# Weight pieces of a hybrid diffusion step: eight 128-row chunks in two buffers instead of four chunks in four

## The chip, the cores and the metric

The kernel runs on one core of a Trainium2 chip. The metric is the device time of one execution in microseconds (us); three runs of the kernel before were timed, and the profile is of a further execution of the same program. About 0.2% of the time is what a measurement of this kernel can tell from no change.

## The reference, cut to what matters

One inference step over two layers. 128 context tokens and 512 latent tokens (640 columns in all) go through the same weights. Each layer multiplies the normalised input by one wide matrix, sends the slices of the result through three kinds of mixer, and multiplies the concatenated results by an output matrix.

```python
mod = jnp.matmul(jax.nn.silu(cond), w_ada) + b_ada
shift, scale, gate = jnp.split(mod[:, None, :], 3, axis=-1)
h = rmsnorm(x, norm_g) * (1 + scale) + shift
proj = jnp.matmul(h, w_in)                       # 2048 -> 7168
q, k, v, ag, lx, lg, hv, hx1, hx0, hg = jnp.split(proj, SPLITS, axis=-1)
...
xc = dwconv(lx, lru_conv_w, lru_conv_b, 2, 1)
h_f = rglru_dir(xc, lru_wa[0], ..., False)       # 64x64 block gates, then a scan
h_b = rglru_dir(xc, lru_wa[1], ..., True)
...
out = jnp.matmul(jnp.concatenate([att, lru, hy], axis=-1), w_out)   # 2048 -> 2048
return x + gate * out, k_store, v_store, h_last
```

## The kernel before, in words

All activations lie transposed: 128 features on the partitions, 640 tokens in the free dimension, sixteen such tiles for 2048 features, each kept as a high and a low part (`A`, type fp32r) so that three matmuls give nearly fp32 precision. TensorE multiplies in fp32r; the weights come from memory as fp32 and are split the same way.

**A weight piece.** `load_w` (L369) fetches four chunks of 128 rows by 128 columns with one DMA of 256 KB into a tile `wr`, ScalarE casts it to fp32r (`wh`, L178), and VectorE subtracts to get the rest (`wl`, L179). `wr`, `wh` and `wl` have four buffers each, in the pool `W` (L145) and by `WR = 4` (L37).

**A projection.** `gemm` (L401) makes one block of 128 output features: over sixteen chunks, that is four pieces, each chunk with three weight/input pairs (`wh` with the high part, `wh` with the low part, `wl` with the high part) in two halves of 320 tokens. So a piece is 24 matmuls and a projection is 96, all at L420. Two PSUM accumulators alternate. Between the pieces the loop may call `hook`, which spreads the next adaLN product over VectorE (L335), and `filt`, which spreads the filter and convolution steps.

**Order.** A scheduler places the instructions of each engine at build time by priority and by its own estimate of when they are ready; every engine then works through its own list in order, and so do the DMA queues (nearly all transfers are issued by SP). The calls of `load_w` in `gemm` and `gemm_parts` stand under `high_priority(offset=600)`, so that a piece is fetched and split ahead of the matmuls that use it. A buffer is given again when its last reader is done: for `wr` that is the subtraction, for `wh` and `wl` the last matmul of the piece.

**Stages**, once per layer: adaLN and normalisation (layer 0: forty smaller pieces of two or four chunks, `gemm_part`, L513, called from L1265); the hyena gates; the RG-LRU (`lru`, L926, four blocks j); attention (`attention`, L1037, eight heads); three attention gates; hyena's inputs, filters and convolutions with the other gates; the output projection (`out_proj`, L1365). Its last two feature blocks, and the first two of the next layer, go through `gemm_parts` (L379), which runs over the tokens in two parts and keeps the pieces of a pool `wz` for both.

**The RG-LRU block** matters below. `lru` makes two projections, LX and LG, then builds the block-diagonal gate weights in a tile of the same tags: GpSimd clears `wr` (L950), four small DMAs fill it (L954), and it is split like a piece (L957). Four sets of six matmuls (L713, through `mm3`) read its `wh` and `wl`: two gates for the forward scan, two for the backward one. They stand between the matmuls of the next projection, since each set waits for ScalarE to empty the one PSUM tile `pS` of the set before (L968).

Of the kernel before, what the change touches and what calls it, by code (L numbers as in the profile page):

```python
# [11 lines left out]
F32 = mybir.dt.float32  # L12
F32R = mybir.dt.float32r
# [20 lines left out]
EPS = 1e-6  # L34
TCE_W = 258
PI = math.pi
WR = 4  # L37
CVB = 3
LEAD = 4
NAT = 4  # L40
# [97 lines left out]
class K:  # L138
    def __init__(self, ctx, tc, i, o, taps=None):
        self.ctx, self.tc, self.nc, self.i, self.o = ctx, tc, tc.nc, i, o  # L140
        self.taps = taps or {}
        nc = tc.nc
        P = lambda name, bufs, **kw: ctx.enter_context(tc.tile_pool(name=name, bufs=bufs, **kw))
        self.cst = P("cst", 1)
        self.W = P("W", 4)  # L145
        self.sm = P("sm", 2)
        self.pm = P("pm", 2, space=PSUM)
        self.hook = self.filt = None
        self.hn = 0
        self.n = 0  # L150
# [215 lines left out]
                nc.vector.scalar_tensor_tensor(mod[:, sl, s], mod[:, sl, s], 1.0, g, op0=ALU.add, op1=ALU.mult)  # L366


    def load_w(self, wd, k, m0, n=4, keep=None):  # L369

        nc = self.nc
        wr = self.tl(self.W, [128, 4, 128], F32, "wr", bufs=WR)[:, :n, :]
        nc.sync.dma_start(wr, wd[k * 128:(k + n) * 128, m0:m0 + 128].rearrange("(c p) m -> p c m", p=128))
        wh = self.tl(keep or self.W, [128, 4, 128], F32R, "wh")[:, :n, :]
        wl = self.tl(keep or self.W, [128, 4, 128], F32R, "wl")[:, :n, :]
        self.split(wh, wl, wr)
        return wh, wl

    def gemm_parts(self, wd, ms, rhs, order, parts, keeps):  # L379

        nc = self.nc
        ps = [self.pm.tile([128, 2, 512], F32, name=self.nm("g_%d" % m), tag="m") for m in ms]
        ws = {}
        yield ps
        for n0, (c0, c1, j, o) in enumerate(parts):
            for a in range(4):
                ks = order[4 * a:4 * a + 4]
                for m, p in zip(ms, ps):
                    if n0 == 0:
                        with self.tc.high_priority(offset=600):  # L390
                            ws[a, m] = self.load_w(wd, ks[0], m, keep=keeps[a])
                        if self.hook is not None:
                            next(self.hook, None)
                    wh, wl = ws[a, m]
                    for c, k in enumerate(ks):
                        for n, (w, x) in enumerate(((wh, 0), (wh, 1), (wl, 0))):
                            nc.tensor.matmul(p[:, j, o:o + c1 - c0], lhsT=w[:, c, :], rhs=rhs[k][x][:, c0:c1],  # L397
                                             start=(a == 0 and c == 0 and n == 0), stop=(a == 3 and c == 3 and n == 2))
                yield

    def gemm(self, wd, ms, rhs, order=range(KC)):  # L401

        nc = self.nc
        ps = [self.pm.tile([128, 2, 512], F32, name=self.nm("g_%d" % m), tag="m") for m in ms]
        for a in range(4):
            ks = order[4 * a:4 * a + 4]
            for m, p in zip(ms, ps):
                with self.tc.high_priority(offset=600):
                    wh, wl = self.load_w(wd, ks[0], m)
                if self.hook is not None:  # L410
                    self.hn += self.hr
                    while self.hn >= 1:
                        self.hn -= 1
                        next(self.hook, None)
                if self.filt is not None and (a + 1) * self.fs // 4 > a * self.fs // 4:
                    next(self.filt, None)
                for c, k in enumerate(ks):
                    for n, (w, x) in enumerate(((wh, 0), (wh, 1), (wl, 0))):
                        for j in range(2):
                            nc.tensor.matmul(p[:, j, :HT], lhsT=w[:, c, :], rhs=rhs[k][x][:, j * HT:(j + 1) * HT],  # L420
                                             start=(a == 0 and c == 0 and n == 0), stop=(a == 3 and c == 3 and n == 2))
        return [p[:, :, :HT] for p in ps]
# [503 lines left out]
    def lru(self, l, hs, j, pool, hl_tile):  # L926
# [19 lines left out]
        xl = self.tl(pool, [128, 644], F32R, tag="lxl")  # L946
        self.split(xh, xl, xc)
        sg = self.silu2(self.proj(l, COL_LG + j * 128, hs), pool, "lsg", 1)
        wr = self.tl(self.W, [128, 4, 128], F32, "wr", bufs=WR)
        nc.gpsimd.memset(wr, 0.0)  # L950
        for gi, nmw in ((0, "lru_wa"), (1, "lru_wi")):
            for bl in range(2):
                s = slice(bl * 64, bl * 64 + 64)
                nc.sync.dma_start(wr[s, 2 * gi:2 * gi + 2, s], i[nmw][l, :, 2 * j + bl].rearrange("d c e -> c d e"))  # L954
        wh = self.tl(self.W, [128, 4, 128], F32R, "wh")
        wl = self.tl(self.W, [128, 4, 128], F32R, "wl")
        self.split(wh, wl, wr)  # L957
        hh = []
        for d in range(2):
# [240 lines left out]
    def run(self):  # L1200
# [12 lines left out]
        with ExitStack() as st, self.tc.tile_pool(name="ps0", bufs=1, space=PSUM) as self.pst:  # L1213
# [12 lines left out]
            hs = []  # L1226
# [34 lines left out]
            for gi, (k0, kn) in enumerate(groups):  # L1261
                more = gi + 1 < len(groups)
                nxt = iter(())
                for n, m0 in enumerate(first):
                    self.gemm_part(self.load_w(w, k0, m0, kn), m0, hs, k0, kn, self.early[0, m0])  # L1265
                    ada_to(done + (2 if kn == 4 or gi else 1))
                    next(nxt, None)
                    if more and n == NAT:
# [96 lines left out]
    def out_proj(self, l):  # L1365
# [3 lines left out]
        self.hr = RATE[l]["out"]  # L1369
        wd, mod, ms = self.i["w_out"][l], self.par[l]["mod"], self.mix  # L1370
        zs = ExitStack()
        zp = zs.enter_context(self.pool("wz", 8))
        st = ExitStack()
        pool = st.enter_context(self.pool("out"))
        acc = self.tl(pool, [128, T], tag="acc")
# [173 lines left out]
```

## Time and profile before

| | |
|---|---|
| median of three runs | 2725.28 us (2720.43 to 2726.11) |
| the profiled execution | 2730.49 us, of which 2728.5 us from first to last instruction |
| TensorE busy / its weight loads | 95% / 91% of the span |
| VectorE / ScalarE / GpSimd busy | 70% / 39% / 10% |
| granted TensorE clock, mean | 0.987 of full speed |
| DMA moved | 354.83 MB, 130 GB/s |

Matmuls are pipelined, so their recorded lengths overlap; the engine's rate is read from the distance between starts. "Idle before" an instruction is the time its engine did nothing ahead of it, and the releaser is whatever ended last of what it waited for. Idle time of an engine that is not the bound costs nothing.

### The profile page before, as it was taken

Reading aid. Unit: us, or ns where it says so; the run is one execution under the profiler, and the core shown is the slowest. Engines: PE = TensorE matmul, PEld = TensorE weight load, DVE = VectorE, ACT = ScalarE, POOL = GpSimd, SP = SyncE. Lnnn points to the kernel's source line nnn. Section 1 sums busy time; section 2 is a strip of 40 time slices with the busy share of each in tenths; the row PEclk is TensorE's granted clock in tenths of the full one; section 3 lists DMA queues with packets and bytes.
Section 4 is the critical chain, followed back from the end, with each engine's and each line's share of the span. In section 5 each row is a group of like instructions: output and inputs, shape, how many; then the busy total and the mean of one; then the engine's idle time right before and its main releaser. Section 6 shows DMA issues by size and latency. Waiting matters only on the chain. (4 is left out here: it accounts for less than half of the span.)

```text
span 2728.5 us, 45802 instructions
## 1 busy us (share of the span) xinstructions
PE 2599.8 (95%) x17503; PEld 2485.5 (91%) x17503; DVE 1920.0 (70%) x3499; ACT 1076.9 (39%) x1970; POOL 261.6 (10%) x352
## 2 busy tenths in 40 slices
PE   4999989999999999989998999999999999999998
PEld 2589989999999998889998999999999999989997
DVE  3568997787888787777679467877777756564333
ACT  4224545455554222132235256444455522223222
POOL 1000220000000221200001012000000021120000
PEclk9999999999999999999999999999999999999999
DMA  8773443332333545576664323422322252345333
GB/s 256 247 239 118 128 136 90 90 106 66 102 93 114 173 136 158 158 227 200 191 196 147 117 69 86 127 87 86 101 75 64 59 166 79 106 143 158 98 94 118
DMA packets 439911, 354.83 MB, mean 130 GB/s; under 512 B 26746, under 2 KB 367618, under 8 KB 439436
## 3 DMA queue, kind: packets, MB, share of 16 engines
q1 hardware_dynamic: 428618, 336.39, 41.1%
q10 hardware_dynamic: 9586, 9.42, 1.1%
q0 software_dynamic: 1488, 6.10, 0.6%
q8 instruction: 137, 2.24, 0.3%
q14 instruction: 82, 0.67, 0.1%
HBM read 316.51 MB, written 35.32 MB: 129 GB/s over the span
## 5 line engine op out<-in xcount | busy, mean ns | idle before, releaser
L420 PE MATMUL g<-A,wh 128*128 128x320 f32 x8320 | 1614.1, 311 | 5.6 <-ACT A L178 5.0
L420 PEld LDWEIGHTS g<-A,wh 128*128 128x128 f32 x8320 | 1321.3, 189 | 7.3 <-ACT A L178 5.3
L420 PE MATMUL g<-A,wl 128*128 128x320 f32 x4160 | 963.9, 310 | 0.0
L178 ACT CAST wh<-wr 128x512 fp32r<-128x512 f32 (+1 forms) x592 | 362.1, 613 | 966.3 <-PE g L420 696.2
L420 PEld LDWEIGHTS g<-A,wl 128*128 128x128 f32 x4160 | 702.6, 189 | 0.2
L179 DVE TENSOR_TENSOR wl<-wr,wh 128x512 fp32r<-128x512 f32 (+1 forms) x592 | 429.2, 728 | 339.0 <-ACT wh L178 323.9
L335 DVE SCALAR_TENSOR_TENSOR adas<-wa,cs,adas 128x512 f32<-128x512 f32 x480 | 363.9, 784 | 61.4 <-DMA wa<-in_w_ada 60.1
L1160 ACT ACTIVATE e<-e,mx 128x768 f32<-128x768 f32 (+1 forms) x160 | 133.7, 835 | 69.2 <-DVE e L1159 68.9
L1159 DVE TENSOR_SCALAR_CACHE_REDUCE e<-pS 128x768 f32<-128x768 f32 (+1 forms) x160 | 131.0, 819 | 9.1 <-PE pS L713 3.9
L1122 POOL TENSOR_TENSOR oq<-ot 128x640 f32<-128x640 f32 x16 | 20.9, 1309 | 912.5 <-ACT ot L1118 689.7
L713 PE MATMUL pS<-kk,qq 128*128 128x384 f32 (+1 forms) x288 | 100.3, 348 | 3.9 <-DVE e L1159 3.4
L521 PE MATMUL gp<-A,wh 128*128 128x320 f32 x512 | 101.9, 318 | 1.0 <-ACT wh L178 1.0
L397 PE MATMUL g<-A,wh 128*128 128x320 f32 (+2 forms) x384 | 92.9, 324 | 8.9 <-DVE A L492 5.9
L521 PEld LDWEIGHTS gp<-A,wh 128*128 128x128 f32 x512 | 79.7, 189 | 23.0 <-issue 11.2
L713 PE MATMUL pS<-kl,qq 128*128 128x384 f32 (+1 forms) x288 | 95.2, 331 | 0.0
L179 DVE TENSOR_TENSOR wtl<-pt,wth 128x512 fp32r<-128x512 f32 (+1 forms) x144 | 70.1, 522 | 29.6 <-ACT wth L178 29.3
L178 ACT CAST wth<-pt 128x512 fp32r<-128x512 f32 (+1 forms) x144 | 59.7, 459 | 61.6 <-PE pt L1103 60.0
L313 PE MATMUL pa<-wada,csw 128*32 128x512 f32 (+1 forms) x320 | 52.7, 565 | 28.9 <-DVE st L436 21.5
L397 PEld LDWEIGHTS g<-A,wh 128*128 128x128 f32 x384 | 67.0, 194 | 14.4 <-DVE A L492 8.3
L1396 DVE SCALAR_TENSOR_TENSOR xf<-g,mod,xo 128x128 f32<-128x128 f32 (+3 forms) x96 | 38.3, 432 | 55.8 <-PE g L420 23.2
L1166 DVE SCALAR_TENSOR_TENSOR e<-e,rz,e 128x768 f32<-128x768 f32 (+1 forms) x80 | 70.6, 882 | 1.7
L713 PEld LDWEIGHTS pS<-kk,qq 128*128 128x128 f32 x288 | 54.0, 187 | 14.7 <-DVE e L1159 8.8
(353 smaller groups left out, 3159.7 us busy)
## 6 DMA issues: line engine op xcount, KB each, us to landing
wr<-in_w_in SPq DMA_DIRECT2D x440, 256.0 KB
wa<-in_w_ada SPq DMA_DIRECT2D x256, 256.0 KB
wada<-in_w_ada SPq DMA_DIRECT2D x64, 512.0 KB
wr<-in_w_out SPq DMA_DIRECT2D x128, 256.0 KB
mx<-md SPq DMA_DIRECT2D x28, 320.0 KB
md<-ot SPq DMA_DIRECT2D x16, 320.0 KB
gm<-md SPq DMA_DIRECT2D x16, 320.0 KB
R<-rd SPq DMA_DIRECT2D x16, 320.0 KB
```

Of the source, the lines that this page charges most:

```text
L178: self.nc.scalar.copy(hi, src)
L179: self.nc.vector.tensor_tensor(lo, src, hi.bitcast(F32), op=ALU.subtract)
L313: nc.tensor.matmul(acc[32 * q:32 * q + 32, :], lhsT=self.csw[:, k, :], rhs=w[:, j, :], start=k < 4, stop=k >= 12, tile_position=(0, 32 * q))
L335: nc.vector.scalar_tensor_tensor(acc[:, s], w, c, acc[:, s], op0=ALU.mult, op1=ALU.add)
L397: nc.tensor.matmul(p[:, j, o:o + c1 - c0], lhsT=w[:, c, :], rhs=rhs[k][x][:, c0:c1], start=(a == 0 and c == 0 and n == 0), stop=(a == 3 an ...
L420: nc.tensor.matmul(p[:, j, :HT], lhsT=w[:, c, :], rhs=rhs[k][x][:, j * HT:(j + 1) * HT], start=(a == 0 and c == 0 and n == 0), stop=(a == ...
L521: nc.tensor.matmul(p[:, j, :HT], lhsT=w[:, c, :], rhs=rhs[k0 + c][x][:, j * HT:(j + 1) * HT], start=(c == 0 and t == 0), stop=(c == n - 1 ...
L713: self.nc.tensor.matmul(out, lhsT=a, rhs=b, start=(n == 0), stop=(n == len(pairs) - 1))
L1159: V.tensor_scalar(e[:, :nk].rearrange("p (a b) -> p a b", a=nhf), ps[:, :nhf, :hw], -1.0, None, op0=ALU.mult, op1=ALU.min, accum_out=mx)
L1160: nc.scalar.activation(e[:, :nk], e[:, :nk], AF.Exp, scale=-1.0, bias=mx, accum_out=Z[:, c:c + 1])
L1166: V.scalar_tensor_tensor(es[0][:, :nk], es[1][:, :nk], rz[:, 1:2], es[0][:, :nk], op0=ALU.mult, op1=ALU.add)
L1396: V.scalar_tensor_tensor(x[:, a:b], p, mod[:, 32 + m, s:s + 1], xo[:, a:b], op0=ALU.mult, op1=ALU.add)
```

## The change

`load_w` takes a list of piece starts and fetches each with a DMA of its own into one tile of eight chunks, then casts and subtracts the whole tile in one instruction each. `gemm` and `gemm_parts` call it at every second piece and hand out halves. The pool `W` has two buffers of eight chunks in place of four of four (the same bytes), and `wz` four in place of eight. The forty early pieces and the RG-LRU's gate weights, which have at most four chunks, now take a part of an eight-chunk buffer each. The calls of `hook` and `filt` stay at every piece of four chunks.

```diff
-WR = 4
-        self.W = P("W", 4)
+        self.W = P("W", 2)
...
-    def load_w(self, wd, k, m0, n=4, keep=None):
+    def load_w(self, wd, ks, m0, n=4, keep=None):
         nc = self.nc
-        wr = self.tl(self.W, [128, 4, 128], F32, "wr", bufs=WR)[:, :n, :]
-        nc.sync.dma_start(wr, wd[k * 128:(k + n) * 128, m0:m0 + 128].rearrange("(c p) m -> p c m", p=128))
-        wh = self.tl(keep or self.W, [128, 4, 128], F32R, "wh")[:, :n, :]
-        wl = self.tl(keep or self.W, [128, 4, 128], F32R, "wl")[:, :n, :]
+        N = n * len(ks)
+        wr = self.tl(self.W, [128, 8, 128], F32, "wr")[:, :N, :]
+        for j, k in enumerate(ks):
+            nc.sync.dma_start(wr[:, j * n:j * n + n, :], wd[k * 128:(k + n) * 128, m0:m0 + 128].rearrange("(c p) m -> p c m", p=128))
+        wh = self.tl(keep or self.W, [128, 8, 128], F32R, "wh")[:, :N, :]
+        wl = self.tl(keep or self.W, [128, 8, 128], F32R, "wl")[:, :N, :]
         self.split(wh, wl, wr)
         return wh, wl
...
     def gemm(self, wd, ms, rhs, order=range(KC)):
+        ws = {}
         for a in range(4):
             ks = order[4 * a:4 * a + 4]
             for m, p in zip(ms, ps):
-                with self.tc.high_priority(offset=600):
-                    wh, wl = self.load_w(wd, ks[0], m)
+                if a % 2 == 0:
+                    with self.tc.high_priority(offset=600):
+                        ws[m] = self.load_w(wd, (ks[0], order[4 * a + 4]), m)
+                wh, wl = (w[:, a % 2 * 4:a % 2 * 4 + 4, :] for w in ws[m])
...
     def lru(self, l, hs, j, pool, hl_tile):
-        wr = self.tl(self.W, [128, 4, 128], F32, "wr", bufs=WR)
+        wr = self.tl(self.W, [128, 8, 128], F32, "wr")[:, :4, :]
-        wh = self.tl(self.W, [128, 4, 128], F32R, "wh")
-        wl = self.tl(self.W, [128, 4, 128], F32R, "wl")
+        wh = self.tl(self.W, [128, 8, 128], F32R, "wh")[:, :4, :]
+        wl = self.tl(self.W, [128, 8, 128], F32R, "wl")[:, :4, :]
...
-                    self.gemm_part(self.load_w(w, k0, m0, kn), m0, hs, k0, kn, self.early[0, m0])
+                    self.gemm_part(self.load_w(w, (k0,), m0, kn), m0, hs, k0, kn, self.early[0, m0])
...
-        zp = zs.enter_context(self.pool("wz", 8))
+        zp = zs.enter_context(self.pool("wz", 4))
```

`gemm_parts` changes as `gemm` does: a load at every even a, halves handed to a and a + 1.

## Rows read from the trace of the kernel before

**Rows 1.** The page, busy time, share of the span and instructions of each engine.

```profile
PE 2599.8 (95%) x17503; PEld 2485.5 (91%) x17503; DVE 1920.0 (70%) x3499; ACT 1076.9 (39%) x1970; POOL 261.6 (10%) x352
```

**Rows 2.** Busy time by stage: RG-LRU 0, attention 0, hyena 0, RG-LRU 1, attention 1.

```profile
core 0: us, PE busy (x) PEld busy (x) DVE busy (x) ACT busy (x) POOL busy (x), PEclk, DMA share, GB/s
256.00:412.00 156.00, 140.58 (x911) 137.96 (x910) 142.12 (x207) 81.03 (x111) 36.02 (x30) 0.95 0.42 125
412.00:886.00 474.00, 467.02 (x3176) 452.67 (x3175) 384.81 (x752) 245.09 (x473) 25.64 (x16) 1.00 0.32 93
886.00:1228.00 342.00, 319.36 (x2164) 310.26 (x2163) 266.55 (x439) 84.99 (x157) 59.38 (x92) 0.98 0.56 171
1592.00:1730.00 138.00, 135.09 (x905) 133.53 (x904) 102.35 (x156) 81.25 (x112) 33.78 (x30) 0.99 0.30 89
1730.00:2190.00 460.00, 452.81 (x3064) 438.19 (x3063) 352.16 (x702) 236.65 (x462) 24.89 (x16) 0.99 0.28 82
```

**Rows 3.** Waits: who waited for whom, us in total, times, longest us.

```profile
ACT wh L178 <- PE g L420: 696.2, 308, 8.5
DVE wl L179 <- ACT wh L178: 323.9, 188, 5.1
...
PE pt L775 <- DVE uS L771: 11.8, 8, 2.3
...
PE g L420 <- ACT A L178: 5.0, 1, 5.0
```

**Rows 4.** Groups by line and form: xcount, busy us, mean ns of one, idle before.

```profile
L179 DVE TENSOR_TENSOR wl<-wr,wh 128x512 fp32r<-128x512 f32 x576 | 422.6, 736 | 332.0 <-ACT wh L178 317.1 <-PE pt L341 8.8 <-DMA wr<-in_w_in 2.5
L178 ACT CAST wh<-wr 128x512 fp32r<-128x512 f32 x576 | 355.6, 619 | 957.2 <-PE g L420 696.2 <-issue 94.5 <-PE gp L521 44.1
...
L179 DVE TENSOR_TENSOR kl<-ks,kk 64x896 fp32r<-64x896 f32 x32 | 34.7, 1085 | 11.8 <-ACT kk L178 11.5
...
L178 ACT CAST kk<-ks 64x896 fp32r<-64x896 f32 x32 | 30.1, 941 | 14.2 <-DVE ks L1035 13.8
```

**Rows 5.** Output projection of layer 1: chain (start, us), then timelines of ACT and DVE.

```profile
2507.02 3.52 PE g L420 x24
...
2532.84 0.62 ACT L178 CAST wh<-wr 128x512 fp32r<-128x512 f32 x1 [2.90 <-PE g L420]
2533.49 0.69 DVE L179 TENSOR_TENSOR wl<-wr,wh 128x512 fp32r<-128x512 f32 x1 [2.83 <-ACT wh L178]
```

**Rows 6.** Timelines of ACT, DVE and PE, one RG-LRU block of layer 1.

```profile
1608.40 0.62 ACT L178 CAST wh<-wr 128x512 fp32r<-128x512 f32 x1 [2.23 <-POOL lt L986]
1612.50 0.69 DVE L179 TENSOR_TENSOR wl<-wr,wh 128x512 fp32r<-128x512 f32 x1
1618.72 0.45 PE L420 MATMUL g<-A,wl 128*128 128x320 f32 x2
1624.86 0.61 ACT L178 CAST wh<-wr 128x512 fp32r<-128x512 f32 x1
1631.45 0.31 PE L713 MATMUL pS<-lxh,wl 128*128 128x322 f32 x1
```

**Rows 7.** The same timelines, last RG-LRU block of layer 0.

```profile
351.83 0.64 ACT L178 CAST wh<-wr 128x512 fp32r<-128x512 f32 x1
360.12 1.28 DVE L179 TENSOR_TENSOR wl<-wr,wh 128x512 fp32r<-128x512 f32 x2
381.75 0.47 PE L713 MATMUL pS<-lxh,wl 128*128 128x322 f32 x1
```

**Rows 8.** Busy time by stretch around one stall of TensorE, columns as in rows 2.

```profile
1718.00:1720.50 2.50, 0.77 (x6) 0.51 (x4) 2.44 (x5) 2.45 (x4) 0.00 (x0) 1.00 0.27 80
1720.50:1723.90 3.40, 3.21 (x13) 3.21 (x13) 3.37 (x10) 0.14 (x1) 0.00 (x0) 0.50 0.33 89
```

**Rows 9.** Early pieces of two chunks: timelines of ACT and SP, then the chain.

```profile
57.98 0.41 ACT L178 CAST wh<-wr 128x256 fp32r<-128x256 f32 x1
58.44 0.42 SPq L373 DMA_DIRECT2D wr<-in_w_in  x1
60.50 0.41 ACT L178 CAST wh<-wr 128x256 fp32r<-128x256 f32 x1
...
2664.80 3.14 DMA wr<-in_w_out
```

More of the change, by code (lines that the diff above doesn't have):

```diff
@@ L389, in gemm_parts @@
                     if n0 == 0:
-                        with self.tc.high_priority(offset=600):
-                            ws[a, m] = self.load_w(wd, ks[0], m, keep=keeps[a])
+                        if a % 2 == 0:
+                            with self.tc.high_priority(offset=600):
+                                w2 = self.load_w(wd, (ks[0], order[4 * a + 4]), m, keep=keeps[a])
+                            for n in range(2):
+                                ws[a + n, m] = [w[:, 4 * n:4 * n + 4, :] for w in w2]
                         if self.hook is not None:
@@ L407, in gemm @@
             for m, p in zip(ms, ps):
-                with self.tc.high_priority(offset=600):
-                    wh, wl = self.load_w(wd, ks[0], m)
+                if a % 2 == 0:
+                    with self.tc.high_priority(offset=600):
+                        ws[m] = self.load_w(wd, (ks[0], order[4 * a + 4]), m)
+                wh, wl = (w[:, a % 2 * 4:a % 2 * 4 + 4, :] for w in ws[m])
                 if self.hook is not None:
```

## The prediction, made before the change was run

> **What bounds the kernel now.** The first view is the busy table of the page: TensorE works 95% of the span, its weight loads 91%, while VectorE has 70% and ScalarE 39% [rows 1]. TensorE sets the time, and a change to ScalarE's and VectorE's work counts only through TensorE's pauses. The second view is the table by stage [rows 2]: attention is nearly full (467.0 of 474 us in layer 0), the hyena stage lacks 22.6 of 342 us, and the RG-LRU of layer 0 is the odd one: TensorE lacks 15.4 of 156 us and VectorE works 142.1. The third is the list of waits [rows 3]. ScalarE stands 696.2 us in front of a weight cast until TensorE releases a buffer, and VectorE 323.9 us until ScalarE has cast; the only wait of the main matmuls listed there is 5.0 us, for an activation and not for a weight. So the weight path runs ahead of TensorE and is throttled by free buffers. The question is what is left of that lead.
>
> **What is removed.** Of 576 splits of 512 columns [rows 4], 24 are early pieces and 8 are gate weights; 544 become 272 of 1024 columns. The price of 1024 columns is not in the trace, so I go on from 512 and 896 columns [rows 4]: the cast rises from 619 to 941 ns, 0.84 ns per column, to about 1.05 us; the subtraction from 736 to 1085 ns, 0.91 per column, to about 1.20 us. Saved per pair are 2 x 0.62 - 1.05 = 0.19 us of ScalarE and 2 x 0.736 - 1.20 = 0.27 us of VectorE, over 272 pairs 51 and 73 us. These are 5% and 4% of what the two engines do. On the path lies only the share by which TensorE's pauses behind them shrink. The two attention stages and hyena 0 lack 7.0, 7.2 and 22.6 us [rows 2] and the largest group of such waits is 11.8 us [rows 3]; 5% of the pauses is 2 us. In the RG-LRU of layer 0, nearly bound by VectorE, some 17 pairs give 17 x 0.27 = 4.6 us. I take -6 us; bounds 0 (all hidden) and -20 (a third of those pauses and of RG-LRU 0's 15.4 us).
>
> TensorE's matmuls are the same in number and kind. Twenty-four take 3.52 us [rows 5], without a seam that a missing wait could close: zero.
>
> **What is added: a later release.** In the output projection a cast begins the moment TensorE leaves a piece, and the subtraction 0.65 us later, so a piece is ready 0.69 + 0.65 = 1.34 us after its release [rows 5]. Four buffers give it the time of three pieces, 10.6 us. After the change the pair is ready 1.05 + 1.20 + 0.15 = 2.4 us after its release, and one pair's matmuls, 7.04 us, cover it. Four matmuls of a piece need `wh` alone, another 0.6 us. The lead falls from 9.2 to 4.6 us plus this 0.6. In pure projections it is enough: zero. In attention TensorE works on scores between the pieces, which only lengthens the cover: zero. The first call of `gemm` in the output projection has two feature blocks at once, and only 3.52 us of cover, still over 2.4: zero. Two DMAs per pair instead of one leave the count and bytes alone; one lands in about 3.1 us [rows 9], and a `wr` buffer has 14 - 2.4 = 11.7 us from its subtraction to its next cast: zero, with that lead as the cover. SP has no more to issue; the waits that it stands in become longer and fewer.
>
> **The buffer that the gate weights hold.** This is the term that I believe in. The gate weights take a whole buffer of `wh` and `wl` from their cast to the last of their four sets: 1608.40 to 1631.45, 23 us, in the block of layer 1 [rows 6], and 351.83 to 381.75, 30 us, in the last one of layer 0 [rows 7]. With four buffers three are left; a cast at 1624.86 proceeds inside that stretch, since any freed buffer is used [rows 6]. With two, one is left, and the projections then run with a single buffer: matmuls, release, cast, subtract, matmuls. Follow one block from the end of its LG projection, 1618.72 + 0.3 = 1619.0. The next pair can be cast only now. TensorE has one set of six gate matmuls (0.9 us) and, after the cast, four matmuls (0.6 us), so it stands 2.4 - 0.6 - 0.9 = 0.9 us. That pair ends at about 2.4 + 44 x 0.147 + two more sets 1.8 = 10.7 us, while the gate buffer comes free at 1631.45 - 1619.0 = 12.5 us or later; so the pair after it waits again, 0.9 us if the fourth set falls there, else 1.8. That is 1.8 to 2.7 us per block with both engines free. They are not: in the block of rows 6 the subtraction starts 3.5 us after its cast ended, and in that of rows 7 it is 7.7 us [rows 6, 7]. I add 0.7 us of queue per stall and take 0.9 + 1.35 (the middle of 0.9 and 1.8) + 2 x 0.7 = 3.7 us a block, 1.85 us a stall.
>
> RG-LRU 1: TensorE is full there (135.1 of 138 us, rows 2), so four blocks cost 15 us. [...] Together +19; bounds 4 (the queues free, one of the two stalls filled by other work) and 45 (eight stalls of 1.1 us behind subtractions late by 3.5 us are 37, and the clock at half of them 7).
>
> RG-LRU 0: the same price, but a stall of TensorE there runs partly beside VectorE's backlog, which would have made TensorE wait anyway. I take +13; bounds 0 (all absorbed) and 45 (at half of the eight stalls subtractions 7.7 us late, 31 us, and 1.85 + 1.7 us at the others, 14).
>
> **The early pieces** of two chunks follow each other at 60.50 - 57.98 = 2.5 us [rows 9]. With two buffers a DMA is issued after the subtraction two pieces earlier, has 2 x 2.5 - 0.9 = 4.1 us, and needs 0.4 + 3.1 and its place behind adaLN's transfers. Eight pieces at up to 0.4 us: +3, bounds 0 and 12, as later early pieces have 3.5 us and more of matmuls for cover.
>
> **The sum**, against the profiled execution: 2730.5 - 6 + 19 + 13 + 3 = 2759.5 us, +29. That execution is 5.2 us above the median of the three runs, 2725.3, so I forecast 2754 us.
>
> **Rivals.** *Faster: what is saved weighs more.* The freed 73 us of VectorE shorten the softmax and hyena chains, and the scheduler, which knows that the next pair comes late, puts gate matmuls and transposes into the holes. For it: VectorE works 81% in attention 0 and 91% in RG-LRU 0. Against it: TensorE's pauses behind both engines are small. It gives -20 + 4 + 0 + 3 = -13, or 2712 us, and decides where the gate buffer's stalls stay under about 10 us in sum. [...]
>
> *No change:* the stalls fall into pauses that are there now, and -6 + 4 + 0 + 3 is +1: 2726 us, if RG-LRU 1's holes are filled.
>
> *Much slower:* a stall is long enough each time that the half clock follows, and late subtractions reach both RG-LRU stages. Sixteen stalls of 1.85 + 1.7 us are 57 us; with 19 us of lateness (4.8 us at four blocks of layer 0) and 3 early, less 6: +73, or 2798 us. The rows for it are the half clock and the 7.7 us [rows 7, 8]. [...]
>
> **How the numbers follow.** The forecast has 0.54 (its own range 2732 to 2780), faster 0.17, no change 0.15, much slower 0.14. What a measurement of this kernel can tell from no change is about 0.2%, 5.5 us. So slower by more is 0.54 + 0.14 = 0.68, within it 0.15, faster 0.17. The range 2712 to 2798 leaves out the lower half of "faster" and the upper half of "much slower", 0.16.
>
> **What would show it.** Right: the large casts take about 1.05 us and the subtractions 1.20; the waits list gains lines of L420's matmuls on the cast and subtraction of weights, nearly all within the two RG-LRU stages; RG-LRU 1 lasts about 19 us longer and RG-LRU 0 about 13; attention and the output projections keep their length within 3 us. Wrong: the stage table shows the same RG-LRU lengths, or the added time lies in attention or hyena (then it is the lead of 4.6 us that was too short), or the large instructions cost more than two small ones.

## The result, and the profile after the change

The changed kernel takes 2773.33 us, the median of four runs (2770.81 to 2776.42), beside 2725.7 us for the kernel before in runs of the same series: a ratio of 1.0179, 95% interval 1.0163 to 1.0196. It is slower by some 48 us; the forecast was 29 us slower, with a range that holds 2773. The profiled execution has a span (first to last instruction) of 2772.6 us against 2728.5, so the 44.1 us between the spans are what the traces can explain.

First the busy table of the page after the change, and its three groups of weight work (line, engine, operation, count | busy us, mean ns of one | idle time before them and what ended most of it). L427 answers to L420 of before, L177 and L178 to L178 and L179, L374 to L373, L334 to L335, L720 to L713.

```profile
PE 2619.6 (94%) x17503; PEld 2497.0 (90%) x17503; DVE 1867.4 (67%) x3227; ACT 1030.7 (37%) x1698; POOL 266.9 (10%) x352
...
L427 PE MATMUL g<-A,wl 128*128 128x320 f32 x4160 | 969.5, 312 | 25.0 <-DVE wl L178 24.9
...
L177 ACT CAST wh<-wr 128x1024 fp32r<-128x1024 f32 (+2 forms) x320 | 311.3, 974 | 850.9 <-PE g L427 614.0
L178 DVE TENSOR_TENSOR wl<-wr,wh 128x1024 fp32r<-128x1024 f32 (+2 forms) x320 | 361.6, 1132 | 244.4 <-ACT wh L177 236.8
```

The work did what the change says: 272 instructions fewer on each of the two engines, VectorE's busy time down from 1920.0 [rows 1] to 1867.4 us and ScalarE's from 1076.9 to 1030.7. The main group of TensorE's matmuls now has a releaser that the page of before did not list: `wl`. The lists of waits after the change say the same (who waited for whom, us in total, times, longest; three lines are of SP's queue, of VectorE and of TensorE alone):

```profile
ACT wh L177 <- PE g L427: 614.0, 168, 9.5
DVE wl L178 <- ACT wh L177: 236.8, 102, 6.8
PE g L427 <- DVE wl L178: 24.9, 14, 3.1
PE g L427 <- ACT wh L177: 1.7, 6, 0.4
DVE adas L334 <- DMA wa<-in_w_ada: 99.9, 68, 3.9
SPq L374 <- DVE wl L178: 830.6, 222, 13.7
```

The first two answer to [rows 3]: the weight path still stands most of the time in front of buffers that TensorE holds. But 26.6 us of the opposite wait have appeared. Two lines of the kernel before, which will be needed, are:

```profile
DVE adas L335 <- DMA wa<-in_w_ada: 60.1, 73, 2.9
SPq L373 <- DVE wl L179: 1045.7, 466, 8.7
```

Where the 44.1 us lie is read from stages. I cut both traces at the same place of the program: a stage runs from the start of its first main matmul to that of the next stage's first one (so the edges are other ones than in rows 2). Busy time by these stages, RG-LRU 0, attention 0, hyena 0, RG-LRU 1, hyena 1; first the kernel before, then the changed one:

```profile
core 0: us, PE busy (x) PEld busy (x) DVE busy (x) ACT busy (x) POOL busy (x), PEclk, DMA share, GB/s
228.20:364.80 136.60, 130.34 (x866) 127.97 (x866) 121.36 (x196) 69.45 (x103) 26.78 (x31) 0.99 0.40 118
364.80:843.60 478.80, 464.38 (x3134) 451.01 (x3134) 387.67 (x740) 242.37 (x453) 32.16 (x20) 0.99 0.33 96
843.60:1178.10 334.50, 312.82 (x2130) 302.50 (x2128) 272.43 (x463) 86.84 (x170) 62.95 (x94) 0.99 0.52 156
1558.90:1684.10 125.20, 125.20 (x848) 124.28 (x848) 83.04 (x119) 67.63 (x98) 25.65 (x28) 1.00 0.28 80
2156.90:2477.10 320.20, 307.66 (x2106) 298.55 (x2105) 192.86 (x336) 85.46 (x169) 55.95 (x94) 0.99 0.39 117
```

```profile
228.30:377.60 149.30, 136.06 (x865) 131.69 (x864) 116.99 (x183) 65.34 (x83) 26.50 (x28) 0.95 0.37 109
377.60:861.70 484.10, 468.69 (x3134) 454.33 (x3135) 370.59 (x675) 236.26 (x404) 32.56 (x20) 0.98 0.31 93
861.70:1199.90 338.20, 313.02 (x2130) 302.83 (x2128) 262.45 (x430) 81.19 (x139) 63.21 (x94) 0.99 0.51 154
1579.80:1721.10 141.30, 131.67 (x857) 128.01 (x855) 101.99 (x139) 65.76 (x82) 25.95 (x28) 0.98 0.34 99
2192.70:2520.20 327.50, 309.69 (x2106) 300.12 (x2105) 185.90 (x306) 80.79 (x139) 56.79 (x94) 0.99 0.38 115
```

RG-LRU 1 is the plainest: TensorE was busy for all of its 125.20 us and is now busy for 131.67 of 141.30. The two RG-LRU stages take 12.7 + 16.1 = 28.8 us more, two thirds of the whole. Attention 0 takes 5.3 more and the two hyena stages 3.7 + 7.3 = 11.0. What is left (attention 1 -1.2, both output projections and layer 1's gates +0.1, the start +0.1) adds up to nothing. So the loss has two parts: 29 us in the two RG-LRU stages, and some 16 us in the others.

The stage edges do not quite part the two. The gate matmuls of the fourth block stand among the first projections of attention, so its gate weights are held beyond the edge, in layer 0 until 391.9 us and in layer 1 until 1732.3 us. TensorE's waits for `wl` in the changed kernel, in RG-LRU 0, attention 0, RG-LRU 1 and attention 1:

```profile
PE g L427 <- DVE wl L178: 9.2, 5, 3.1
PE g L427 <- DVE wl L178: 4.8, 2, 2.9
PE g L427 <- DVE wl L178: 9.3, 5, 2.9
PE g L427 <- DVE wl L178: 1.6, 2, 1.2
```

The two of attention 0 end at 381.3 and 396.1 us, the two of attention 1 at 1722.4 and 1735.3. These four lists are all of the 14 waits and 24.9 us: every wait for `wl` belongs to one of the eight RG-LRU blocks, one to the first block of each layer and two to each of the others.

One stall of RG-LRU 1, from the timeline after the change (start, length, engine, line; idle time before it and who ended it):

```profile
1642.38 1.05 ACT L177 CAST wh<-wr 128x1024 fp32r<-128x1024 f32 x1 [1.15 <-PE g L427]
1642.40 1.40 DVE L334 SCALAR_TENSOR_TENSOR adas<-wa,cs,adas 128x512 f32<-128x512 f32 x2
1642.43 0.30 PE L720 MATMUL pS<-lxh,wh 128*128 128x322 f32 x1
...
1643.49 0.85 PE L427 MATMUL g<-A,wh 128*128 128x320 f32 x4
1644.67 1.41 DVE L334 SCALAR_TENSOR_TENSOR adas<-wa,cs,adas 128x512 f32<-128x512 f32 x2 [0.87 <-DMA wa<-in_w_ada]
1646.00 1.22 DVE L178 TENSOR_TENSOR wl<-wr,wh 128x1024 fp32r<-128x1024 f32 x1
1647.28 0.56 PE L427 MATMUL g<-A,wl 128*128 128x320 f32 x2 [2.94 <-DVE wl L178]
...
1650.22 0.47 PE L720 MATMUL pS<-lxl,wh 128*128 128x322 f32 x1
```

The gate weights have one buffer of `wh` and `wl`. The LG projection ends, the other buffer comes free, and at 1642.38 the next pair can be cast at last. TensorE does one set of gate matmuls from 1642.43 and the four matmuls that need only `wh`, and then stands 2.94 us for `wl`. The cast and the subtraction cost 1.05 and 1.22 us, as forecast; what made the subtraction late is in VectorE's list, where four adaLN products (L334) stand ahead of it, two of them after a wait for their own transfer. From 1.2 us after the stall the granted clock is 0.50 for 3.4 us, in which the gate matmuls start 0.27 us apart (six from 1649.14) in place of the 0.147 us between main matmuls at 1.00 (24 in 3.52 us, rows 5):

```profile
1648.50:1651.90 3.40, 3.40 (x15) 3.40 (x14) 3.37 (x7) 0.89 (x2) 0.00 (x0) 0.50 0.83 240
```

### The profile page after: what moved, and what is told of

It reads as the page before. It is cut to its first block, busy times and chain, and to the rows that moved or that the text cites. A ratio compares the mean times of both kernels' runs of the same rounds, so it can differ in the third digit from the quotient of the medians.

```text
span 2772.6 us, 44843 instructions
## 1 busy us (share of the span) xinstructions
PE 2619.6 (94%) x17503; PEld 2497.0 (90%) x17503; DVE 1867.4 (67%) x3227; ACT 1030.7 (37%) x1698; POOL 266.9 (10%) x352
## 5 line engine op out<-in xcount | busy, mean ns | idle before, releaser
L427 PE MATMUL g<-A,wh 128*128 128x320 f32 x8320 | 1624.1, 312 | 11.9 <-ACT A L177 9.6
L427 PEld LDWEIGHTS g<-A,wh 128*128 128x128 f32 x8320 | 1327.6, 190 | 18.6 <-ACT A L177 10.1
L427 PE MATMUL g<-A,wl 128*128 128x320 f32 x4160 | 969.5, 312 | 25.0 <-DVE wl L178 24.9
L427 PEld LDWEIGHTS g<-A,wl 128*128 128x128 f32 x4160 | 703.9, 190 | 29.3 <-DVE wl L178 29.0
L177 ACT CAST wh<-wr 128x1024 fp32r<-128x1024 f32 (+2 forms) x320 | 311.3, 974 | 850.9 <-PE g L427 614.0
L178 DVE TENSOR_TENSOR wl<-wr,wh 128x1024 fp32r<-128x1024 f32 (+2 forms) x320 | 361.6, 1132 | 244.4 <-ACT wh L177 236.8
L334 DVE SCALAR_TENSOR_TENSOR adas<-wa,cs,adas 128x512 f32<-128x512 f32 x480 | 367.5, 793 | 100.3 <-DMA wa<-in_w_ada 99.9
L720 PE MATMUL pS<-kk,qq 128*128 128x384 f32 (+1 forms) x288 | 102.5, 356 | 4.9 <-DVE e L1166 4.8
L720 PE MATMUL pS<-kl,qq 128*128 128x384 f32 (+1 forms) x288 | 96.0, 333 | 0.0
L178 DVE TENSOR_TENSOR wtl<-pt,wth 128x512 fp32r<-128x512 f32 (+1 forms) x144 | 70.3, 522 | 34.1 <-ACT wth L177 33.6
L177 ACT CAST wth<-pt 128x512 fp32r<-128x512 f32 (+1 forms) x144 | 59.5, 456 | 58.8 <-PE pt L1110 57.5
L720 PEld LDWEIGHTS pS<-kk,qq 128*128 128x128 f32 x288 | 54.5, 189 | 15.9 <-DVE e L1166 13.5
```

The costliest lines, as they stand in the source:

```text
L177: self.nc.scalar.copy(hi, src)
L178: self.nc.vector.tensor_tensor(lo, src, hi.bitcast(F32), op=ALU.subtract)
L334: nc.vector.scalar_tensor_tensor(acc[:, s], w, c, acc[:, s], op0=ALU.mult, op1=ALU.add)
L720: self.nc.tensor.matmul(out, lhsT=a, rhs=b, start=(n == 0), stop=(n == len(pairs) - 1))
```

## The experiments

Five theories were put to the chip, named by a letter in what was expected. **H**: the gate weights hold one of two buffers, so the projections beside them run on a single one. **S**, the rival: it is the size of the pieces (or of the instructions), whatever else holds a buffer. **L**, a second rival: one pair (or piece) of lead is too short by itself, everywhere. **Q**: the length of a stall is set by the adaLN products ahead of the subtraction in VectorE's list. **P**: what is left outside the RG-LRU comes from SP's queue, where other transfers stand behind those of weights. The table has the differences of stage lengths to the kernel before, cut as above, in us of the one profiled execution. The edits are told at the runs.

| kernel | median, us | RG-LRU 0 | RG-LRU 1 | attention 0 / 1 | hyena 0 / 1 |
|---|---|---|---|---|---|
| changed | 2773.3 | +12.7 | +16.1 | +5.3 / -1.2 | +3.7 / +7.3 |
| changed, gates apart | 2751.3 | +3.0 | +0.3 | +4.6 / -4.9 | +7.3 / +5.2 |
| changed, split in halves | 2789.2 | +9.4 | +18.2 | +8.2 / +6.1 | +5.4 / +8.6 |
| small pieces, two buffers | 2780.3 | +13.4 | +23.7 | +1.2 / -1.9 | +6.8 / +1.6 |
| the same, gates apart | 2750.8 | +3.1 | +4.3 | -0.5 / -2.3 | +6.8 / +5.5 |
| the same, four raw buffers | 2743.3 | +2.9 | +4.6 | -0.2 / -0.4 | +2.2 / +3.1 |
| small pieces, three buffers | 2736.0 | +1.5 | 0.0 | +0.4 / +0.4 | +1.0 / +1.9 |
| before, gates apart | 2732.0 | +1.7 | +11.5 | -0.5 / -4.6 | -1.7 / +0.1 |
| changed, no adaLN in RG-LRU 1 | 2769.9 | +8.5 | +9.8 | +5.8 / -1.1 | +7.7 / +3.1 |
| before, no adaLN in RG-LRU 1 | 2723.3 | +0.1 | 0.0 | 0.0 / -0.2 | -0.6 / +2.3 |
| changed, gates apart, GpSimd's queue | 2763.2 | +3.0 | +0.3 | +4.6 / -1.2 | +12.9 / +12.0 |
| before, GpSimd's queue | 2738.6 | 0.0 | 0.0 | +0.2 / +0.9 | +6.7 / +4.6 |
| changed, gates apart, priority 300 | 2745.7 | +2.6 | +0.3 | +3.5 / -3.0 | +5.1 / +6.5 |

**The gate weights in tiles of their own**, in the changed kernel; the edit stands in `lru`, and `pool` is that stage's own.

```diff
-        wr = self.tl(self.W, [128, 8, 128], F32, "wr")[:, :4, :]
-        wh = self.tl(self.W, [128, 8, 128], F32R, "wh")[:, :4, :]
-        wl = self.tl(self.W, [128, 8, 128], F32R, "wl")[:, :4, :]
+        wr = self.tl(pool, [128, 4, 128], F32, "gr")
+        wh = self.tl(pool, [128, 4, 128], F32R, "gh")
+        wl = self.tl(pool, [128, 4, 128], F32R, "gl")
```

> The changed kernel, with the RG-LRU's gate weights in buffers of their own instead of one of the two of pool W. Theory H (the gate weights hold one of two buffers): the two RG-LRU stages go back to their length of before within 4 us each, that is about 25 to 30 us of the added 48 come back, 2744 to 2750 us; what is left (about 18 us) lies in attention and hyena. Rival S (the larger instructions: casts of 1.0 us and subtractions of 1.2 us block ScalarE's and VectorE's lists): little comes back, 2765 us or more. Rival L (one pair of lead is too short anywhere): the RG-LRU stages get back half or less, 2755 to 2770 us.

Measured: 2751.32 us, ratio 1.009 (1.0073 to 1.0107). Busy time of RG-LRU 1 in this kernel, and its list of TensorE's waits over the whole span:

```profile
1578.00:1703.50 125.50, 125.50 (x847) 124.21 (x846) 75.70 (x102) 65.48 (x81) 24.09 (x26) 1.00 0.27 79
```

```profile
PE g L427 <- DVE wl L178: 3.7, 6, 1.1
```

TensorE is full in RG-LRU 1 again, 125.50 of 125.50 us, and of the 24.9 us of waits for `wl` 3.7 are left. Of 28.8 us in the RG-LRU stages 25.5 have come back by moving three tiles, with pieces as large as in the changed kernel and buffers as few. H holds there, each stage being within 4 us of its old length. In all 22.0 us of the 48 came back by the medians, and 2751.3 lies 1.3 us above the range that H gave.

**The same move in the kernel before**, as a control: the same three lines with `[128, 4, 128]`.

> The kernel before with buffers of their own for the gate weights: the control for the first run. All theories: no change from the kernel before within 0.3%, 2718 to 2733 us, since three of four buffers left no stall. If it is faster by more, the gate weights cost time before, too.

Measured: 2732.02 us, ratio 1.0028 (1.0012 to 1.0044). The move is no gain by itself. RG-LRU 1 got 11.5 us longer, though no buffer is short, and attention 1 4.6 shorter. TensorE had no wait in this stage before; now its gate matmuls wait there, most of all for their input `lxh`:

```profile
PE pS L713 <- ACT lxh L178: 4.3, 2, 2.8
```

That the scheduler lists them earlier because their weights are ready earlier is a guess. This is a warning for the table: a new order of the lists alone moves a stage by several us, so differences of 2 or 3 us in one stage of one execution are not read.

**Buffers or size: small pieces in two buffers.** The kernel before with `WR = 2` and two buffers of four chunks in `W`; a pool of four, `wk`, for the two blocks whose pieces `gemm_parts` keeps, which otherwise would wait for each other for ever.

```diff
-WR = 4
+WR = 2
-        self.W = P("W", 4)
+        self.W = P("W", 2)
...
+        kp = zs.enter_context(self.pool("wk", 4))
-        g = self.gemm_parts(self.i["w_in"][1], first, hs, range(KC), ((0, HT, 0, 0), (HT, T, 1, 0)), [None, None, zp, zp])
+        g = self.gemm_parts(self.i["w_in"][1], first, hs, range(KC), ((0, HT, 0, 0), (HT, T, 1, 0)), [kp, kp, zp, zp])
```

> The kernel before, with its four-chunk pieces, but two buffers in place of four (the four pieces that must be kept in the projection between the layers get a pool of their own). Instructions as before, cover of one piece 3.52 us instead of 7.04. Theories H and L: the RG-LRU stages lengthen as in the changed kernel, by 20 to 35 us together (a stall for every piece inside the hold, each shorter), and attention by 5 to 20 us more since 3.52 us of cover is less than many subtractions are late: 2755 to 2785 us. Rival S: as before within 10 us, 2720 to 2736 us.

Measured: 2780.28 us, ratio 1.02 (1.0173 to 1.0226). TensorE's wait for the subtraction in this kernel:

```profile
PE g L420 <- DVE wl L179: 37.1, 27, 3.4
```

The small instructions of before with two buffers lose more in the RG-LRU (37.1 us against 28.8) than the large ones, so the loss needs no large piece or instruction, and S is out for the RG-LRU. That the list above has 37.1 us too is chance: it is of the whole span. The longer attention that had been expected, by 5 to 20 us, did not come (+1.2 and -1.9). Pieces of eight chunks in three buffers were not run.

**Three small buffers** (`WR = 3`, `P("W", 3)`, else as the last run):

> The kernel before with three buffers of four chunks in place of four (kept pieces in a pool of their own, as in the run with two). Theory H: while the gate weights hold one, two are left, and one piece of matmuls (3.52 us) covers a split ready after 1.34 us; so the loss is a fraction of that with two buffers: the RG-LRU stages together 4 to 15 us over the kernel before (two small buffers: 37), 2730 to 2745 us in all. Rival (any smaller number of buffers costs in proportion, whatever holds them): about half of the loss with two buffers in every stage, 2745 to 2760 us.

Measured: 2736.03 us, ratio 1.0053 (1.0037 to 1.007), with 2.4 us of waits for `wl` in 4 places. With two buffers left beside the one that the gate weights hold, the RG-LRU stages lose 1.5 us where one left over lost 37.1, and H had allowed 4 to 15. Between two and three lies nearly everything.

**Two small buffers, gates apart** (the last but one and the first edit together):

> Two buffers of four chunks, as run before, with buffers of their own for the gate weights. Theory H: most of the 37 us in the RG-LRU stages go, 0 to 15 stay, since no one holds a buffer: 2735 to 2755 us. Rival L (one piece of lead is too short by itself): the RG-LRU stages keep 22 us or more of the 37, 2760 us or more.

Measured: 2750.82 us, ratio 1.0102 (1.0082 to 1.0122). Of 37.1 us in the RG-LRU 7.4 are left. H holds for small pieces too, and L does not in the RG-LRU. As with large ones, some 17 us outside the RG-LRU stay, 8.1 of them in output projection 0 and layer 1's gates.

**The split in halves.** The changed kernel, with two casts and two subtractions of 512 columns for each pair.

```diff
-        self.split(wh, wl, wr)
+        for j in range(0, N, n):
+            self.split(wh[:, j:j + n, :], wl[:, j:j + n, :], wr[:, j:j + n, :])
```

> The changed kernel, with its eight-chunk buffers, but cast and subtracted in two halves of 512 columns each, as many instructions as before. Theory H: a half is ready 1.34 us after the release instead of 2.4, so the stalls shrink but do not vanish: 2750 to 2762 us, and the waits of the projection's matmuls for weights fall from 26 us to some 5 to 15. Rival S: nearly all of the loss comes back, 2726 to 2740 us. Rival L: as the changed kernel within 8 us, 2765 to 2780.

Measured: 2789.19 us, ratio 1.0224 (1.0202 to 1.0247), slower than with one instruction, and none of the theories had said so. The waits for `wl` are 23.3 us in 13 places, where H had put 5 to 15: the long instruction was not what made them, and H's reckoning of a stall from the time of cast and subtraction fails here. The buffers are still held and released by pairs. Why it lost 16 us more was not settled; most of it shows in attention 1 (+7.3 us over the changed kernel) and around output projection 0 (+6.3).

**No adaLN products in RG-LRU 1.** `RATE` sets how many of them `hook` places in each stage; the products themselves are all done, in other stages.

```diff
-RATE = (dict(lru=1, att=.5, ag1=.75, hv=.75, ag2=1, out=1), dict(gate=.5, lru=.5, att=.5, ag1=.5, hv=.5, ag2=0, out=0))
+RATE = (dict(lru=1, att=.5, ag1=.75, hv=.75, ag2=1, out=1), dict(gate=.5, lru=0, att=.5, ag1=.5, hv=.5, ag2=0, out=0))
```

> The changed kernel, with no adaLN steps among the projections of the RG-LRU of layer 1 (the same 64 steps, taken later). Theory Q (a stall is as long as VectorE's list ahead of the subtraction, where two to four adaLN steps of 0.7 us stand): the waits for weights in that stage fall from 9.7 us to 3 to 6, their mean from 2 us to about 1, no half clock follows, and the stage takes 129 to 135 us instead of 141.3; in all 4 to 10 us less than the changed kernel. Rival (the stall is the cast and subtraction themselves): the stage stays at 138 to 143 us.

Measured: 2769.9 us, ratio 1.0175 (1.0152 to 1.0197). RG-LRU 1 and TensorE's waits in it, in this kernel:

```profile
1580.10:1715.10 135.00, 128.21 (x849) 124.24 (x847) 74.83 (x103) 65.38 (x82) 23.97 (x28) 1.00 0.25 73
```

```profile
PE g L427 <- DVE wl L178: 4.9, 6, 1.3
```

The stage falls from 141.3 to 135.0 us, the waits for `wl` from 9.3 us (longest 2.9) to 4.9 (longest 1.3), and the granted clock stays at 1.00. So Q holds for the waits: the held buffer makes the stall, and the products listed ahead of the subtraction make it long; with two of the long ones (2.94 and 2.44 us) a spell of 3.4 us at a granted clock of 0.50 had come. With the two waits behind the stage's edge each block has two, one of 0.4 and one of 1.2 to 1.3 us, and 9.8 us of the stage's 16.1 stay without the products. The 6.3 us gained are to be read with care: RG-LRU 0, which the edit leaves alone, is 4.2 us shorter than in the changed kernel too. The total cannot be told from that of the changed kernel (ratios 1.0175 and 1.0179); the 4 to 10 us less that Q had put did not show.

The control, the same edit in the kernel before:

> The control of the run without adaLN steps: the same move of steps in the kernel before. All theories: RG-LRU 1 is full of matmuls already, so its length falls only by the transposes moved, 0 to 2 us; in all within 0.3% of the kernel before, 2717 to 2733 us.

Measured: 2723.27 us, ratio 1.0002 (0.999 to 1.0015), and no RG-LRU stage moved by more than 0.1 us. With four buffers the products cost nothing there.

**SP's queue (theory P).** What pointed to it is this stretch of hyena 0, SP and VectorE after the change, and then the same work before it:

```profile
1097.66 0.94 SPq L374 DMA_DIRECT2D wr<-in_w_in  x2
...
1098.69 0.45 SPq L1018 DMA_DIRECT2D R<-rd  x1
...
1104.23 0.83 DVE L1019 TENSOR_TENSOR gm<-gm,R 128x640 f32<-128x640 f32 x1 [3.09 <-DMA R<-rd]
```

```profile
1076.86 0.38 SPq L1011 DMA_DIRECT2D R<-rd  x1
...
1078.42 0.38 SPq L373 DMA_DIRECT2D wr<-in_w_in  x1
...
1082.20 0.83 DVE L1012 TENSOR_TENSOR gm<-gm,R 128x640 f32<-128x640 f32 x1 [0.97 <-DMA R<-rd]
```

The transfer of `R` now stands behind two weight transfers, which were released by a subtraction, and VectorE waits 3.09 us for it in place of 0.97. In the first try the loads of `m`, `R`, `gm`, `yy` and `g` go by GpSimd's queue, in the changed kernel with the gates apart and, as control, in the kernel before (eight lines, of which one stands here):

```diff
-        nc.sync.dma_start(R, self.rd[l][c:c + 1, :].to_broadcast([128, T]))
+        nc.gpsimd.dma_start(R, self.rd[l][c:c + 1, :].to_broadcast([128, T]))
```

> The changed kernel with the gate weights in tiles of their own, and besides with the loads of m, R, gm, yy and g of the hyena stages issued by GpSimd's queue in place of SP's. Theory P (what is left outside the RG-LRU comes from SP's queue: the transfers of R, gm and yy stand behind weight transfers that wait for a subtraction, and the wait for a pair is longer than that for a piece): the six hyena-side stages, 654.8 us before, 665.7 after the change and 667.2 with the gate weights apart, return to 654 to 660, and the total falls from 2751 to 2738 to 2745. Rival theory (the larger instructions in VectorE's and ScalarE's lists, or only another order of the lists): they stay at 664 to 669, total 2748 to 2754.

> Control: the kernel before with the same loads issued by GpSimd's queue. Theory P: SP's queue costs little here since its waits are short, so the six hyena-side stages stay at 650 to 656 us and the total at 2717 to 2730. Rival: if the move by itself changes these stages by as much as it does in the other run, the gain there says nothing of the change.

Measured: 2763.24 us (ratio 1.0136, 1.0112 to 1.016) and 2738.6 us (1.0047, 1.0028 to 1.0066). Both got slower, by 11.9 us (from 2751.32) and by 0.47%, and in the hyena stages by about the same: 24.9 us over before where the gates apart had 12.5, and 11.3 us in the control. Neither theory's numbers came. VectorE's waits for `gm`, `yy` and `R` did not get shorter by the move (in the control 34.3 us in sum, 27.2 before): the test exchanged one queue's lateness for another's and says nothing on P.

The second try leaves the queue and changes what its weight transfers wait for: two small buffers with the gates apart, but four raw buffers.

```diff
-WR = 2
+WR = 4
```

> Small pieces with two wh and wl buffers and the gate weights in tiles of their own, as in an earlier run (2750.8 us), but with four raw buffers wr in place of two, so that SP's weight transfers wait for an older subtraction. Theory P (SP's queue holds other transfers up behind weight transfers that wait for a subtraction): what stays outside the RG-LRU shrinks by half or more, total 2733 to 2742 us, and SP's wait on weight subtractions gets shorter. Rival theory (two wh and wl buffers leave too little lead in time, whatever the raw buffers are): total 2747 to 2754 us.

Measured: 2743.29 us, ratio 1.0069 (1.0052 to 1.0086), between the two forecasts. The hyena stages lose 5.3 us where they lost 12.3 with two raw buffers, as P says, but not by the way that P tells. SP's wait on the subtractions did not get shorter (8.5 us at the longest, as with two), and VectorE's waits for `R`, from which P was read, are 6.9 us in the hyena stages, 6.3 with two raw buffers. What did go in hyena 0 is a wait of 1.8 us of TensorE for a weight cast. The interval touches that of the run with two raw buffers, and the profiled execution, 2755.3 us, is the slowest of its runs, with 14.3 us more than before in output projection 0 and layer 1's gates. So this run does not show P.

For the pairs, one transfer behind a pair is seen to cost TensorE time, at the end of hyena 1. The changed kernel, then the one before:

```profile
2514.45 2.10 SPq L1367 DMA_DIRECT2D mx<-md  x4
...
2519.41 1.55 ACT L177 CAST A<-mx 128x640 fp32r<-128x640 f32 x2 [1.55 <-DMA mx<-md]
...
2520.18 1.17 PE L427 MATMUL g<-A,wh 128*128 128x320 f32 x3 [3.72 <-ACT A L177]
```

```profile
2468.92 0.38 SPq L1360 DMA_DIRECT2D mx<-md  x1
```

The output projection's inputs (`mx`, cast to `A`) were issued from 2468.92 on, 8.2 us ahead of its first matmul. After the change they stand behind the two transfers of a pair, which waited 2.8 us for VectorE, and come 5.7 us ahead; ScalarE's cast waits for them and TensorE 3.72 us for the cast, half of what hyena 1 lost. In all six kernels with pairs this wait is 2.2 to 4.1 us, in all eight with small pieces it is none. So the rows point to a pair in SP's queue for some of hyena 1; no run took it away. In hyena 0 no such share is shown, and two small buffers lose there as much as pairs, part of it by weights that are late (4.3 us of waits with the gates apart) where with pairs none are.

**An accident of the order?** The changed kernel with the gates apart and another priority for the weight loads, which leaves instructions and buffers alone:

```diff
-                    with self.tc.high_priority(offset=600):
+                    with self.tc.high_priority(offset=300):
```

> The changed kernel with the gate weights in tiles of their own and the scheduler's priority offset of the weight loads 300 in place of 600: the same instructions and buffers, a few matmuls in another order. If what is left outside the RG-LRU (some 20 us) is an accident of the order of the lists, the stages concerned (attention 0, the gate stage of hyena 0, hyena 1, output projection 0) move by several us each and the total by more than 5 us from 2751. If it comes from the two buffers, the total stays at 2747 to 2756 us and these stages within 2 us each.

Measured: 2745.69 us, ratio 1.008 (1.0063 to 1.0097). The median moved by 5.6 us, but not where the rest lies: attention 0 still loses 3.5 us (4.6 with the other priority) and the hyena stages 11.6 (12.5). By what had been put ahead, the total speaks for an accident (more than 5 us) and the stages speak against it. So some us of the total are order; the 15 us in these stages did not go with this other order, the only one tried.

**Attention 0** was left to the traces. It is longer by 3.5 to 8.2 us in each of the six kernels with pairs and by at most 1.2 in the seven others with small pieces (two, three or four buffers), the large instructions or halves alike. Attention 1 is not longer, but for the kernel with halves. In the changed kernel the largest new waits of attention 0 are the 4.8 us for `wl` of the last RG-LRU block, shown above. With the gates apart they are gone, and the stage is still 4.6 us longer than before, so something else is in it. One thing that pairs do there is seen further on in the changed kernel:

```profile
737.04 1.05 ACT L177 CAST wh<-wr 128x1024 fp32r<-128x1024 f32 x1 [2.08 <-PE g L427]
...
739.97 1.41 DVE L334 SCALAR_TENSOR_TENSOR adas<-wa,cs,adas 128x512 f32<-128x512 f32 x2 [2.45 <-DMA wa<-in_w_ada]
741.30 1.22 DVE L178 TENSOR_TENSOR wl<-wr,wh 128x1024 fp32r<-128x1024 f32 x1
742.44 0.28 DVE L1095 COPY vf<-pt 128x128 f32<-128x128 f32 x1
...
742.77 0.41 PE L720 MATMUL pt<-oh,onesr 128*128 128x320 f32 x1 [2.39 <-DVE vf L1095]
```

No weight is late at this place. A copy of 0.28 us that the attention needs (`vf`) stands in VectorE's list behind two adaLN products, which wait for a transfer, and behind the subtraction of a pair; TensorE stands 2.39 us, and the granted clock is 0.50 for 3.4 us from 744.0. With the gates apart the same wait is 2.92 us. Before, the copy at this place follows a reduction of the attention itself and nobody waits:

```profile
724.90 0.95 DVE L1159 TENSOR_SCALAR_CACHE_REDUCE e<-pS 128x768 f32<-128x768 f32 x1
...
725.77 0.29 DVE L1088 COPY vf<-pt 128x128 f32<-128x128 f32 x1
```

In the kernel with halves, where attention 0 lost most, this wait is missing. So the lump is a part of attention 0's loss with pairs; what the rest is stays open, and no experiment took the lump away.

No version ran faster than the kernel before: the best of those with the change's edit or fewer buffers, three small ones, is 0.5% slower.

## Why the prediction was right, and where it was not

- **Sign and size.** Slower was forecast with 0.68, by 29 us; it was 48 by the medians and 44.1 by the spans. The result lies inside the range, and 7 us inside the upper edge of the forecast's own range (2780).
- **The buffer held by the gate weights**, "the term that I believe in": +19 and +13 us forecast, +16.1 and +12.7 measured in the traces, 28.8 in place of 32. Moving three tiles gives 25.5 of them back, and the same kind of loss comes with small pieces in two buffers. The mechanism is shown.
- **Its working** was two stalls of 1.85 us in each of eight blocks, sixteen and 29.6 us. The list has fourteen and 24.9 us, hence 1.78 us on average, and up to 3.1; they lie where the working put them, at the blocks, the last block's beyond the stage's edge. Without adaLN products in layer 1 all eight stalls of that layer are there, 1.6 to 1.7 us a block, where the working had 1.8 to 2.7 with both engines free. The long ones are made by products ahead of the subtraction, for which I had put 0.7 us. That a stall follows from the time of cast and subtraction is not borne out: in halves they were no shorter in sum (23.3 us).
- **Luck in the stage lengths.** RG-LRU 1 has 9.3 us of these waits for the 15 forecast, two spells of 3.4 us at a granted clock of 0.50 (3.4 us lost if the rate falls with the clock, an estimate), and some 3 us that were in no term, to make +16.1. For such spells the +19 holds 4 us, and other sums 1.7 us each. No run shows that loss by itself; from the 0.27 and 0.147 us between matmuls it is 1.5 us a spell, an estimate too. RG-LRU 0 was to have 13 us with no clock in it. It has 9.2 us of the waits, 2.7 of another, and three spells at half clock (13.7 us long, at a clock of 0.50) where before had one of 3.4, which by the clock, an estimate, is 5.1 us more lost; 5.7 us of waits of before are gone. That the sum comes to 12.7 is chance in part.
- **Prices.** 1.05 and 1.22 us for cast and subtraction of 1024 columns, forecast 1.05 and 1.20. VectorE saved 52.6 us and ScalarE 46.2, forecast 73 and 51; the median subtraction of before took 0.69 us, and I had reckoned with the mean, 0.736. The bound of -20 us was added up wrongly: a third of the pauses named, 36.8 + 15.4 us, is 17.4.
- **The step that failed** is the zeros outside the RG-LRU: "In attention TensorE works on scores between the pieces, which only lengthens the cover: zero", the zero for the DMAs, and with them the sign that attention keeps its length within 3 us. Of the -6 us, 4.6 were for RG-LRU 0, so the RG-LRU stages had 19 + 13 - 4.6 = 27.4 us and got 28.8, while the others had -1.4 + 3 = +1.6 and got 44.1 - 28.8 = +15.3, nearly all in attention 0 and the hyena stages. So 14 of the 15 us by which the forecast was short are missing there. I asked only whether a piece is ready in time for its own matmuls. For that the zero was nearly right: with the gates apart 3.7 us of such waits are left in the whole kernel. What I did not ask is who stands behind a pair in the lists of VectorE and SP. The rows show two that do so, the copy in attention 0 (2.39 us of wait and 3.4 us at half clock) and the inputs of output projection 1 (3.72 us). Some of attention 0 is also the last gate buffer, held past the edge of the stage. The rest, hyena 0 above all, is open.
- **SP's waits** for subtractions did become fewer and longer, 222 of up to 13.7 us in place of 466 of up to 8.7. VectorE's wait for adaLN's transfers, which go by SP's queue too, rose from 60.1 to 99.9 us; what that cost TensorE was not measured by itself.
- **Early pieces**: +3 forecast, the first projection starts at 228.3 in place of 228.2 us. The cover held.
- **Rivals.** "Faster" had the saved time on its side; it is real and nobody waited for it. Over the span VectorE had 70% and ScalarE 39% [rows 1], and no gain came. "Much slower" was right in its means, half clock (0.50) after some stalls, as those of 2.94 and 2.44 us in RG-LRU 1, and late subtractions, with waits of up to 3.1 us, and too large: the half clock did not follow each stall (not the one of 2.71 us in RG-LRU 0), and two of sixteen stalls did not come.

## What to carry to other kernels

The same bytes in fewer, larger buffers are not the same lead: count what a long-lived tile of the same tag leaves over, and where that is one buffer, load, split and use become a single file (here 28.8 us in the two RG-LRU stages). Before merging small instructions on engines that are not the bound, look at who stands behind them in each in-order list, the DMA queue's too; a lump can be late for its neighbours even when it is early for its own reader, as in two places here (2.39 and 3.72 us of TensorE's time). Where a held tile's users reach past the edge of a stage, so does its cost: place the waits themselves, and not only the stage lengths. The cheap mend is to take the long-lived tile out of the shared pool (here 22.0 of 48 us came back), and to compare it with the unchanged kernel with the same move.

## What the runs showed that was not expected

- Two buffers to three is a step and no slope: 37.1 us of loss in the RG-LRU stages, then 1.5.
- Two instructions of 512 columns in place of one of 1024, in the same buffers, made the kernel 16 us slower (2789.2 against 2773.3 us).
- A stall of 2.94 us of TensorE was followed by 3.4 us at a granted clock of 0.50, and one of 2.39 us by as long a spell; six waits of at most 1.3 us in RG-LRU 1 without adaLN products were followed by none, RG-LRU 1 staying at 1.00. The length of the stall alone does not decide it: after one of 2.71 us in RG-LRU 0, which ended at 312.19, the clock stayed at 1.00 until 337.8.
- Eight kinds of loads moved from SP's queue to GpSimd's made the kernel before slower by 0.47% and the changed one with the gates apart by 11.9 us, with no other line of the kernels changed.
